# Attention logits on 64 rows of the array: products of hi of q and lo of k for two chunks of keys side by side

## The chip, the cores and the metric

The kernel runs on one core of a Trainium2 chip. The metric is the device time of one launch in microseconds (us). The kernel before takes 1200.92 us, the median of three runs (1200.59 to 1203.84). The engines have short names below: PE is TensorE's matmul and PEld its load of weights, DVE is VectorE, ACT is ScalarE, POOL is GpSimd, SP is SyncE, which only issues transfers here.

## What is computed

One layer of a decoder trunk on x of 1024 tokens by 1024 channels, float32: a norm, one projection, a gated spatial mixer on 4 groups of channels, a dilated causal attention on 12 heads of width 64, an output projection with a residual, and then a convolutional gated MLP. The attention is what the change touches. Cut to what matters:

```
logits = einsum('bnirhd,bnjrhd->bnrhij', qb, kc) * scale + bias      # scale = 1/8
logits = where(mask, logits, NEG_INF)
lse    = logsumexp(logits);  p = exp(logits - lse);  o = einsum(p, vc)
...                                                                  # three (window, dilation) pairs
o = sum(softmax(stack(lses)) * stack(outs))
```

The three dilated segments of a head share their logits, so the kernel works with one causal 1024 by 1024 matrix of logits per head, to which it adds one table that holds the position bias and the logarithm of how many segments contain each distance (-1e30 for none).

## The kernel before

**Numbers in two parts.** Float32 products run on TensorE in a rounded 32-bit type. To keep accuracy, each operand is split in two parts, hi (the rounded value) and lo (the rest), and a product is made of hi*hi, hi*lo and lo*hi, accumulated in one PSUM bank. For the logits the width of a head is only 64, so the array's 128 rows hold both parts of q at once: the tile Q has hi of q (times 1/8) in partitions 0 to 63 and lo of q in partitions 64 to 127. Kh has hi of k in both halves, Kl has lo of k in both halves. One matmul of Q with Kh gives hi*hi + lo*hi, one of Q with Kl gives hi*lo + lo*lo.

**One head.** `proj_qk` makes q and k of a head from the weights of both, 48 matmuls of 512 columns in two halves of 24 (tokens 0 to 511, then 512 to 1023). Behind each half `evac` takes PSUM apart: ScalarE writes hi of k (L483) and hi of q (L484), VectorE lo of k (L485) and lo of q (L486), and SP copies the k parts from partitions 64 to 127 into partitions 0 to 63 (L488, L489). The logits are made by `qk_row` for one block b of 128 queries against its 128*(b+1) keys: in one chunk up to block 3, in two chunks (`CH`) from block 4 on. A chunk has a PSUM bank of its own from a pool of three (`bS`), two matmuls (L511 with Kh, L512 with Kl), and then VectorE adds the bias and takes the running minimum of the negated row (L515). ScalarE takes the exponential (L520), VectorE the reciprocal of the sum (L522), POOL scales the row (L523). `tpv` transposes the rows (L543), splits them in hi and lo (L547 on ScalarE, L548 on VectorE) and multiplies with v (L565).

**Order.** TensorE and SP run in the order in which the code is written. The other engines' lists are put in order by a scheduler when the program is built, so code written for TensorE can move their rows too. A head is done in four steps g = 0 to 3. Each step issues one group of logits, two blocks (`qk_group`: group 0 is blocks 0 and 1, and so on to blocks 6 and 7), then the last product with v of the step before, then `tpv`. Groups 1, 2 and 3 of head h come in its steps 0, 1 and 2; group 0 of head h+1 comes in step 3 of head h. Between the pieces of `tpv`, `pump` issues matmuls of the next head's projection, in numbers from the table `FILL` (11, then 4+6+3, then 3+7+2+4, then 0+3+2+1+2), so the second half of head h's evacuation stands at the end of head h-1, just ahead of group 1 of head h, and the 11 projection matmuls come between group 1 and group 2.

**Buffers.** Q, Kh and Kl of all heads come from four buffers of 1024 columns (tag `qk`). The split weights of q and k (`wqh`, `wql`) have four buffers each of 512 columns, two per head; ScalarE makes the hi part and POOL the lo part.

Of the kernel before, what the change touches and what calls it, by code (L numbers as in the profile page):

```python
# [25 lines left out]
F = mybir.dt.float32  # L26
R = mybir.dt.float32r
# [5 lines left out]
T = 1024  # L33
# [29 lines left out]
def build(tc, x, g1, g2, g3, g4, w_in, ln_g, ln_b, sp_w, sp_b, rel, w_out, w_gate, w_up,  # L63
          conv_w, conv_b, w_down, onehot, lnm, out):
    nc = tc.nc
    pe, act, dve, pool, sp = nc.tensor, nc.scalar, nc.vector, nc.gpsimd, nc.sync
# [4 lines left out]
    def split(hi, lo, src, hi_eng, lo_eng):  # L71
        if hi_eng is act:
            act.activation(hi, src, AF.Copy)  # L73
        elif hi_eng is pool:
            pool.tensor_scalar(hi, src, 1.0, None, op0=OP.mult)
        else:
            dve.tensor_copy(hi, src)
        lo_eng.tensor_sub(lo, src, hi.bitcast(F))  # L78
# [6 lines left out]
    def open_pool(key, **kw):  # L85
        cms[key] = tc.tile_pool(name=key, **kw)
        return cms[key].__enter__()
# [4 lines left out]
    with tc.manual_schedule(engines={ET.PE, ET.SP}), \  # L92
# [8 lines left out]
        def bank(tag, n, nm):  # L101
            return ps.tile([128, 512], F, tag=tag, name=nm, bufs=n)

        def bS(nm):
            return bank("S", 3, nm)
# [7 lines left out]
        def bD(nm):  # L113
            return bank("D", 2, nm)
# [7 lines left out]
        def raw(nm):  # L122
            return rp.tile([128, 1024], F, tag="raw", name=nm)

        def stat(nm, n=1):
            return stp.tile([128, 4], F, tag="st", name=nm)[:, :n]
# [105 lines left out]
        def proj_a(key, n, i, nm, mid=None):  # L232
            p = bD(nm)
            s = slice(i * 128, (i + 1) * 128)
            for k in range(KT):
                if k == (6 if i == 0 else 4) and mid is not None:
                    mid()
                wh, wl = WT[key, k // 2]
                wh, wl = wh[:, k % 2, :], wl[:, k % 2, :]
                pe.matmul(p[:, :n], hTv(i, k, 0), wh, start=k == 0, stop=False)  # L240
                pe.matmul(p[:, :n], hTv(i, k, 0), wl, start=False, stop=False)  # L241
                pe.matmul(p[:, :n], hTv(i, k, 1), wh, start=False, stop=k == KT - 1)  # L242
            return p
# [77 lines left out]
        for i in range(NT):  # L321
# [23 lines left out]
            p = proj_a("uv", 512, i, "uv%d" % i, mid)  # L345
# [70 lines left out]
        for i in range(NT):  # L416
            p = proj_a("v0", 384, i, "v0_%d" % i)
# [18 lines left out]
        ap = open_pool("ag", bufs=2, reuse_waits="tile")  # L436
        WQ, QK, BIAS, ROW = {}, {}, {}, {}

        def load_qk(h):
            r = raw("wqk%d" % h)  # L440
            rv = r.rearrange("p (k c) -> p k c", k=KT)
            for j, nm in enumerate("qk"):
                c0 = C0[nm] + h * 64
                sp.dma_start(rv[:, :, j * 64:(j + 1) * 64],
                             w_in[:, c0:c0 + 64].rearrange("(k p) c -> p k c", p=128))
            WQ[h] = []
            for s in range(2):
                wh = ap.tile([128, 512], R, tag="wqh", name="wqh%d_%d" % (h, s), bufs=4)
                wl = ap.tile([128, 512], R, tag="wql", name="wql%d_%d" % (h, s), bufs=4)
                split(wh, wl, r[:, s * 512:(s + 1) * 512], ENG[WQK_HI[s]], pool)  # L450
                WQ[h].append((wh, wl))

# [7 lines left out]
        def proj_qk(h):  # L460
            st = {}

            def mm(hf, k, j):
                def f():
                    if k == 0 and j == 0:
                        st[hf] = bD("qk%d_%d" % (h, hf))
                    wh, wl = WQ[h][k // 4]
                    c = slice((k % 4) * 128, (k % 4 + 1) * 128)
                    w = wl[:, c] if j == 2 else wh[:, c]
                    m = hT[hf, k // 2, j == 1][:, k % 2, :]  # L470
                    pe.matmul(st[hf], w, m, start=k == 0 and j == 0, stop=k == KT - 1 and j == 2)  # L471
                    if k == KT - 1 and j == 2:
                        evac(hf)
                return f

            def evac(hf):
                if hf == 0:
                    QK[h] = tuple(ap2.tile([128, T], R, tag="qk", name="%s%d" % (n, h), bufs=4)
                                  for n in ("Q", "Kh", "Kl"))
                q, kh, kl = QK[h]  # L480
                p = st[hf]
                s = slice(hf * 512, (hf + 1) * 512)
                act.activation(kh[64:128, s], p[64:128], AF.Copy)  # L483
                act.activation(q[0:64, s], p[0:64], AF.Copy, scale=0.125)  # L484
                dve.tensor_sub(kl[64:128, s], p[64:128], kh.bitcast(F)[64:128, s])  # L485
                dve.scalar_tensor_tensor(q[64:128, s], p[0:64], 0.125, q.bitcast(F)[0:64, s],  # L486
                                         op0=OP.mult, op1=OP.subtract)
                sp.dma_start(kh.bitcast(F)[0:64, s], kh.bitcast(F)[64:128, s])  # L488
                sp.dma_start(kl.bitcast(F)[0:64, s], kl.bitcast(F)[64:128, s])  # L489

            return [mm(hf, k, j) for hf in range(2) for k in range(KT) for j in range(3)]

# [6 lines left out]

        CH = {4: (256, 384), 5: (384, 384), 6: (384, 512), 7: (512, 512)}  # L500

        def qk_row(h, b):
            q, kh, kl = QK[h]
            w = 128 * (b + 1)
            t = ap2.tile([128, T], F, tag="row", name="row%d_%d" % (h, b), bufs=4)
            c0 = 0
            nm = 3.0e38
            for n in CH.get(b, (w,)):
                p = bS("s%d_%d_%d" % (h, b, c0))
                qs = q[:, b * 128:(b + 1) * 128]  # L510
                pe.matmul(p[:, :n], qs, kh[:, c0:c0 + n], start=True, stop=False)  # L511
                pe.matmul(p[:, :n], qs, kl[:, c0:c0 + n], start=False, stop=True)  # L512
                nn = stat("nm%d_%d_%d" % (h, b, c0))
                o = 128 * (7 - b) + c0
                dve.tensor_tensor_reduce(t[:, c0:c0 + n], p[:, :n], BIAS[h][:, o:o + n], -1.0, nm,  # L515
                                         op0=OP.add, op1=OP.min, accum_out=nn)
                nm = nn
                c0 += n
            z = stat("z%d_%d" % (h, b))
            act.activation(t[:, :w], t[:, :w], AF.Exp, bias=nm, scale=-1.0, accum_out=z)  # L520
            rz = stat("rz%d_%d" % (h, b))
            dve.reciprocal(rz, z)  # L522
            pool.tensor_scalar(t[:, :w], t[:, :w], rz, 1.0, op0=OP.mult, op1=OP.mult)  # L523
            ROW[h, b] = t

        def qk_group(h, g):
            qk_row(h, 2 * g)
            qk_row(h, 2 * g + 1)

        def tpv(h, g, nfill):  # L530
            pair, odd = divmod(h, 2)
# [49 lines left out]

        bias_copies(0)
        load_qk(0)
        load_bias(0)
        for i in range(NT):
            p = proj_a("v1", 384, i, "v1_%d" % i)
            v_out(1, i, p)
            if i == 0:
                load_qk(1)
                bias_copies(1)  # L590
                bias_copies(2)
        close_pool("sa")
        ap2 = open_pool("ag2", bufs=4, side="right", reuse_waits="tile")
# [32 lines left out]
        fill.extend(proj_qk(0))  # L626
        pump(48)
        qk_group(0, 0)
        fill.extend(proj_qk(1))
        
        last_pv = lambda: None
        for h in range(HEADS):
            if h + 1 < HEADS:
                load_bias(h + 1)
            if h + 2 < HEADS:
                load_qk(h + 2)
# [5 lines left out]
            for g in range(4):  # L642
                if g < 3:
                    qk_group(h, g + 1)
                elif h + 1 < HEADS:
                    qk_group(h + 1, 0)
                if h == HEADS - 2:
                    if g == 0:
                        m0 = [mtile("ms0_%d" % s, R).rearrange("p (k c) -> p k c", k=KT) for s in range(2)]
                        mix_split(0, m0[0], m0[1], range(KT - 1))  # L650
                    for k in WO_AT[g]:
                        load_wo(k)
                if h == 0 and g == 0:
                    pump(FILL_FIRST)
                last_pv()
                last_pv = tpv(h, g, FILL_AT.get(h, FILL)[g])
                if g == 3 and h + 2 < HEADS:
                    fill.extend(proj_qk(h + 2))
                if g == 3 and h == HEADS - 2:
                    pump(len(fill))  # L660
                    for k in WO_AT[4]:
                        load_wo(k)
# [574 lines left out]
```

## Time and profile before

| | before |
|---|---|
| median of three runs | 1200.92 us (1200.59 to 1203.84) |
| the profiled execution | 1203.99 us, its span 1202.3 us, granted clock 0.992 |
| PE busy | 1160.8 us, 97% of the span |
| DVE busy | 841.0 us, 70% |
| ACT busy | 582.2 us, 48% |
| POOL busy | 380.2 us, 32% |
| logits matmuls | 144 of L511 and 144 of L512, from 159.8 to 451.5 us |
| one head, 180 to 350 us | 24.3 to 24.7 us |

How to read it: times in the timeline are start and duration in us from the start of the span. A busy PE is not PE at its peak: matmuls are pipelined, each shows a duration that overlaps the next one's start, so the distance between two starts is what a matmul costs. A remark in square brackets at the end of a row says how long the engine had been idle and what ended that.

### The profile page before, as it was taken

To read this page: it belongs to the slowest core of one execution; us is meant where nothing else is said; L and a number is where in the kernel's file an instruction comes from. 1 tells how busy PE (TensorE), PEld (TensorE's weight loads), DVE (VectorE), ACT (ScalarE), POOL (GpSimd) and SP (SyncE) were. 2 spreads that over 40 slices of the span, in tenths; PEclk is the share of its full clock that TensorE was granted. 3 is DMA by queue.
4 is the path that set the end of the run, shared out by engine and by line. 5 is a ranking of instruction groups with operands and counts; after the bars stand their busy time and mean duration, and the time that the engine had idled before them with its cause. 6 is when DMAs were issued, how large, how long until landed. Compare 5 with 4: busy or idle time off the path is not lost.

```text
span 1202.3 us, 16542 instructions
## 1 busy us (share of the span) xinstructions
PE 1160.8 (97%) x5687; PEld 975.2 (81%) x5687; DVE 841.0 (70%) x1559; ACT 582.2 (48%) x1172; POOL 380.2 (32%) x401
## 2 busy tenths in 40 slices
PE   6899999999999999998999999999999999999996
PEld 4789978888887878886778888888888888888884
DVE  5862257777777785468797777767777679679665
ACT  4532256666766665366443343433444245445521
POOL 3850023334323374234433223331233310000342
PEclk9999999999999999999999999999999999999999
DMA  5313032343233342341133314332243279334336
GB/s 194 108 59 101 13 83 73 91 118 82 73 77 79 104 141 71 109 154 53 35 116 113 98 69 131 103 126 76 91 132 96 86 281 371 107 97 120 112 116 227
DMA packets 107562, 134.83 MB, mean 112 GB/s; under 512 B 30794, under 2 KB 74326, under 8 KB 107478
## 3 DMA queue, kind: packets, MB, share of 16 engines
q1 hardware_dynamic: 105318, 131.93, 35.4%
q10 hardware_dynamic: 2160, 1.84, 0.4%
q8 instruction: 45, 0.74, 0.2%
q14 instruction: 39, 0.32, 0.1%
HBM read 98.82 MB, written 35.71 MB: 112 GB/s over the span
## 4 chain that ended last, share of the span: by engine, by line
PE 84%; DVE 6%; DMA 3%; POOL 2%; ACT 2%; issue 1%; SPq 1%; POOLq 0%; DVEq 0%; ACTq 0%
PE d L988 15%; PE qk L471 10%; PE y L622 7%; PE o L565 4%; PE pt L543 4%; PE s L511 2%; PE v L240 2%; PE s L512 2%; PE v L242 2%; PE v L241 2%; PE Bu L847 2%; PE Bu L849 2%; PE Bu L848 2%; PE Bg L849 2%; PE Bg L847 2%; PE Bg L848 2%
## 5 line engine op out<-in xcount | busy, mean ns | idle before, releaser
L988 PE MATMUL d<-t,s 128*128 128x512 f32 x924 | 210.4, 389 | 1.5 <-ACT t L73 1.2
L988 PEld LDWEIGHTS d<-t,s 128*128 128x128 f32 x924 | 173.3, 188 | 38.3 <-ACT t L73 1.6
L523 POOL TENSOR_SCALAR row<-row,rz 128x128 f32<-128x128 f32 (+3 forms) x96 | 73.1, 762 | 212.7 <-DVE rz L522 200.8
L520 ACT ACTIVATE row<-row,nm 128x128 f32<-128x128 f32 (+3 forms) x96 | 74.4, 775 | 48.6 <-DVE nm L515 48.3
L548 DVE TENSOR_TENSOR ptl<-pt,pth 128x512 fp32r<-128x512 f32 (+1 forms) x120 | 75.8, 634 | 19.3 <-ACT pth L547 17.9
L622 PE MATMUL y<-woh,ms 128*128 128x512 f32 x256 | 82.8, 396 | 0.4 <-DVE Q L486 0.4
L547 ACT ACTIVATE pth<-pt 128x512 fp32r<-128x512 f32 (+1 forms) x120 | 65.8, 550 | 33.3 <-PE pt L543 32.2
L471 PE MATMUL qk<-hTh,wqh 128*128 128x512 f32 x192 | 80.9, 421 | 0.0
L73 ACT ACTIVATE s<-sf 128x512 fp32r<-128x512 f32 x77 | 48.3, 627 | 66.1 <-PE d L988 26.2
L471 PE MATMUL qk<-hTl,wqh 128*128 128x512 f32 x192 | 78.7, 410 | 0.0
L471 PE MATMUL qk<-hTh,wql 128*128 128x512 f32 x192 | 76.6, 399 | 0.0
L78 DVE TENSOR_TENSOR s<-sf,s 128x512 fp32r<-128x512 f32 x77 | 56.4, 733 | 22.9 <-ACT s L73 22.8
L1003 POOL TENSOR_TENSOR x<-x,g4t 128x512 f32<-128x512 f32 x12 | 18.9, 1591 | 162.3 <-DMA g4t<-in_norm_ffn_post 133.5
L543 PE MATMUL pt<-ident,row 128*128 128x128 f32 x432 | 68.4, 274 | 1.7 <-POOL row L523 1.5
L73 ACT ACTIVATE wtg<-tg 128x512 fp32r<-128x512 f32 x44 | 27.6, 630 | 80.0 <-PE Cu L849 67.6
L797 POOL TENSOR_TENSOR tu<-wu 128x512 f32<-128x512 f32 x11 | 15.3, 1388 | 149.3 <-PE Ag L849 75.5
L900 DVE SCALAR_TENSOR_TENSOR c<-G,cols,c 128x1023 f32<-128x1023 f32 (+1 forms) x44 | 57.7, 1327 | 6.7 <-ACT c L898 6.7
L515 DVE CUSTOM_DVE_ANT_0 row<-s,bias 128x384 f32<-128x384 f32 (+2 forms) x96 | 49.9, 519 | 17.7 <-PE s L512 12.4
L73 ACT ACTIVATE wtu<-tu 128x512 fp32r<-128x512 f32 x44 | 27.6, 630 | 67.5 <-PE Cg L849 50.8
L543 PEld LDWEIGHTS pt<-ident,row 128*128 128x128 f32 x432 | 51.2, 140 | 10.6 <-POOL row L523 2.7
L622 PEld LDWEIGHTS y<-woh,ms 128*128 128x128 f32 x256 | 47.9, 188 | 10.8 <-issue 0.8
L565 PE MATMUL o<-ptl,V 128*128 128x256 f32 x240 | 49.5, 288 | 4.8 <-DVE ptl L548 4.6
(338 smaller groups left out, 3238.6 us busy)
## 6 DMA issues: line engine op xcount, KB each, us to landing
sf<-sD SPq DMA_DIRECT2D x77, 256.0 KB, 2.8
wu<-in_w_up SPq DMA_DIRECT2D x11, 1024.0 KB, 5.1
wd<-in_w_down SPq DMA_DIRECT2D x22, 512.0 KB, 7.2
wg<-in_w_gate SPq DMA_DIRECT2D x10, 1024.0 KB, 5.9
sD<-c SPq DMA_DIRECT2D x30, 256.0 KB, 6.6
gcop<-gd SPq DMA_DIRECT2D x12, 576.0 KB, 4.9
wqk<-in_w_in SPq DMA_DIRECT2D x24, 256.0 KB, 6.0
bias<-gcop SPq DMA_DIRECT2D x12, 512.0 KB, 3.8
```

The lines of the kernel that those rows point to most:

```text
L73: act.activation(hi, src, AF.Copy)
L78: lo_eng.tensor_sub(lo, src, hi.bitcast(F))
L471: pe.matmul(st[hf], w, m, start=k == 0 and j == 0, stop=k == KT - 1 and j == 2)
L520: act.activation(t[:, :w], t[:, :w], AF.Exp, bias=nm, scale=-1.0, accum_out=z)
L523: pool.tensor_scalar(t[:, :w], t[:, :w], rz, 1.0, op0=OP.mult, op1=OP.mult)
L543: pe.transpose(p[:, a * 128:(a + 1) * 128], r[:, jj * 128:(jj + 1) * 128], ident)
L547: act.activation(hi[:, :n], p[:, :n], AF.Copy)
L548: dve.tensor_sub(lo[:, :n], p[:, :n], hi.bitcast(F)[:, :n])
L565: pe.matmul(ov, v, t[:, s], start=j == 0 and x == 0, stop=x == 1 and j == 2 * g + 1, skip_group_check=True)
L622: pe.matmul(YP[i, hf], m, w, start=k == 0 and j == 0, stop=k == KT - 1 and j == 2)
L900: dve.scalar_tensor_tensor(c[:, d:T], g[:, 0:T - d], col(2 - d, f), c[:, d:T], op0=OP.mult, op1=OP.add)
L988: pe.matmul(b, l, r, start=first and n in FIRST and q == 0, stop=last and n in LAST and q == 2, skip_group_check=True)
```

## The change

The second matmul of a chunk now multiplies hi of q with lo of k alone; the product of lo of q and lo of k is left out. It needs only 64 of the array's rows. For two chunks the full matmuls with Kh come first, one behind the other, and then the two small ones: the first chunk's with rows 0 to 63, the second's with rows 64 to 127. For that there is a fourth tile per head, KQ: lo of k in partitions 0 to 63 and hi of q in partitions 64 to 127. The first chunk takes hi of q from Q and lo of k from KQ, the second takes hi of q from KQ and lo of k from Kl. The two chunks are the two blocks of a group for groups 0 and 1, and the two chunks of a block for groups 2 and 3.

SP now issues three copies per half of the evacuation instead of two: hi of k as before, lo of k into KQ, and hi of q into KQ. The buffers of tag `qk` go from four to five, those of `wqh` and `wql` from four to three each. All sizes of chunks, the fill table and the number of matmuls are as before.

```diff
-                wh = ap.tile([128, 512], R, tag="wqh", name="wqh%d_%d" % (h, s), bufs=4)
-                wl = ap.tile([128, 512], R, tag="wql", name="wql%d_%d" % (h, s), bufs=4)
+                wh = ap.tile([128, 512], R, tag="wqh", name="wqh%d_%d" % (h, s), bufs=3)
+                wl = ap.tile([128, 512], R, tag="wql", name="wql%d_%d" % (h, s), bufs=3)
...
-                    QK[h] = tuple(ap2.tile([128, T], R, tag="qk", name="%s%d" % (n, h), bufs=4)
-                                  for n in ("Q", "Kh", "Kl"))
-                q, kh, kl = QK[h]
+                    QK[h] = tuple(ap2.tile([128, T], R, tag="qk", name="%s%d" % (n, h), bufs=5)
+                                  for n in ("Q", "Kh", "Kl", "KQ"))
+
+                q, kh, kl, kq = QK[h]
...
                 sp.dma_start(kh.bitcast(F)[0:64, s], kh.bitcast(F)[64:128, s])
-                sp.dma_start(kl.bitcast(F)[0:64, s], kl.bitcast(F)[64:128, s])
+                sp.dma_start(kq.bitcast(F)[0:64, s], kl.bitcast(F)[64:128, s])
+                sp.dma_start(kq.bitcast(F)[64:128, s], q.bitcast(F)[0:64, s])
...
+        def qk_mm(h, jobs):
+            q, kh, kl, kq = QK[h]
+            ps_ = []
+            for b, c0, n in jobs:
+                p = bS("s%d_%d_%d" % (h, b, c0))
+                pe.matmul(p[:, :n], q[:, b * 128:(b + 1) * 128], kh[:, c0:c0 + n], start=True, stop=False)
+                ps_.append(p)
+            for (b, c0, n), p, x, y, r in zip(jobs, ps_, (q, kq), (kq, kl), (slice(0, 64), slice(64, 128))):
+                pe.matmul(p[:, :n], x[r, b * 128:(b + 1) * 128], y[r, c0:c0 + n], start=False, stop=True)
+            return ps_
...
-            for n in CH.get(b, (w,)):
-                p = bS("s%d_%d_%d" % (h, b, c0))
-                qs = q[:, b * 128:(b + 1) * 128]
-                pe.matmul(p[:, :n], qs, kh[:, c0:c0 + n], start=True, stop=False)
-                pe.matmul(p[:, :n], qs, kl[:, c0:c0 + n], start=False, stop=True)
+            for n, p in zip(CH.get(b, (w,)), ps_):
...
         def qk_group(h, g):
-            qk_row(h, 2 * g)
-            qk_row(h, 2 * g + 1)
+            bs = (2 * g, 2 * g + 1)
+            if g < 2:
+                ps_ = qk_mm(h, [(b, 0, 128 * (b + 1)) for b in bs])
+                for b, p in zip(bs, ps_):
+                    qk_row(h, b, [p])
+                return
+            for b in bs:
+                n0, n1 = CH[b]
+                qk_row(h, b, qk_mm(h, [(b, 0, n0), (b, n0, n1)]))
```

The second matmuls of a chunk stand at L514 in the changed kernel, the first ones at L511 as before. On the engines whose lists the scheduler orders, rows move too. On VectorE, around the first chunk of group 3 (row_6 is its first block, ptl_1_1 the lo part of the transposed rows of group 1), before:

```order
L515 ISA row_6_2652,nm_6_0_2656<-s_6_0_2653,bias_2175 128x384
L515 ISA nm_6_0_2656 128x1
L548 TENSOR_TENSOR ptl_1_1_2633<-pt_1_1_2628,pth_1_1_2632 128x384
L515 ISA row_6_2652,nm_6_384_2661<-s_6_384_2658,bias_2175,nm_6_0_2656 128x512
L515 ISA nm_6_384_2661 128x1
```

and now:

```order
L565 TENSOR_TENSOR ptl_1_1_2645<-pt_1_1_2640,pth_1_1_2644 128x384
L525 ISA row_6_2672,nm_6_0_2673<-s_6_0_2666,bias_2184 128x384
L525 ISA nm_6_0_2673 128x1
L525 ISA row_6_2672,nm_6_384_2675<-s_6_384_2668,bias_2184,nm_6_0_2673 128x512
L525 ISA nm_6_384_2675 128x1
```

The copy to ptl stands ahead of the block's first chunk instead of between its two chunks. On POOL the second of the two lo parts of the weights (wql_1) moves from ahead of block 6's scaling to behind it, ahead of block 7's:

```order
L78 TENSOR_TENSOR wql_0_2511<-wqk_2507,wqh_0_2510 128x512
L78 TENSOR_TENSOR wql_1_2515<-wqk_2507,wqh_1_2514 128x512
L523 TENSOR_SCALAR row_6_2652<-row_6_2652,rz_6_2665 128x896
L523 TENSOR_SCALAR row_7_2668<-row_7_2668,rz_7_2681 128x1024
```

and now:

```order
L78 TENSOR_TENSOR wql_0_2523<-wqk_2519,wqh_0_2522 128x512
L533 TENSOR_SCALAR row_6_2672<-row_6_2672,rz_6_2679 128x896
L78 TENSOR_TENSOR wql_1_2527<-wqk_2519,wqh_1_2526 128x512
L533 TENSOR_SCALAR row_7_2688<-row_7_2688,rz_7_2695 128x1024
```

Its counterpart on ScalarE, the hi part, moves the same way. The lists of TensorE and SP are shown in the prediction, at the places that it speaks of.

More of the change, by code (lines that the diff above doesn't have):

```diff
@@ L500, in build, with qk_row @@
         CH = {4: (256, 384), 5: (384, 384), 6: (384, 512), 7: (512, 512)}
-        def qk_row(h, b):
-            q, kh, kl = QK[h]
+        def qk_mm(h, jobs):
[8 more added lines that the diff above has]
+            return ps_
+        def qk_row(h, b, ps_):
             w = 128 * (b + 1)
```

## The prediction

> **What bounds the kernel now.** I read the page first, then the busy times of single heads, then one head's instructions in order of time. The first row is the page's; the two below it are from the view by stretches, each cut from one head's first logits matmul to the next head's.
>
> ```profile
> PE 1160.8 (97%) x5687; PEld 975.2 (81%) x5687; DVE 841.0 (70%) x1559; ACT 582.2 (48%) x1172; POOL 380.2 (32%) x401
> ...
> 204.87:229.47 24.60, 24.60 (x150) 21.25 (x149) 18.00 (x51) 17.09 (x37) 8.69 (x11) 1.00 0.37 89
> 229.47:253.80 24.33, 24.33 (x150) 21.19 (x149) 17.95 (x50) 16.86 (x36) 8.34 (x10) 1.00 0.36 90
> ```
>
> A head takes 24.3 to 24.6 us, TensorE is covered for all of it at full clock, and VectorE has work for 18.0. So time saved on TensorE is saved, and each wait that TensorE takes on is lost. The change touches four places of a head, its groups 0 to 3 of logits. Here are rows of groups 1 to 3 of one head from the timeline:
>
> ```profile
> 235.35 0.34 PE L511 MATMUL s<-Kh,Q 128*128 128x384 f32 x1
> ...
> 236.18 0.34 PE L565 MATMUL o<-pth,V 128*128 128x256 f32 x2
> ...
> 237.34 0.46 SPq L489 DMA_DIRECT2D Kl<-Kl  x1
> ...
> 237.85 0.58 SPq L456 DMA_DIRECT2D bias<-gcop  x1
> ...
> 239.46 0.28 PE L511 MATMUL s<-Kh,Q 128*128 128x256 f32 x1
> ...
> 239.58 0.28 PE L512 MATMUL s<-Kl,Q 128*128 128x256 f32 x1
> ...
> 239.70 0.34 PE L511 MATMUL s<-Kh,Q 128*128 128x384 f32 x1
> ...
> 239.88 0.33 PE L512 MATMUL s<-Kl,Q 128*128 128x384 f32 x1
> ...
> 240.01 0.42 DVE L515 CUSTOM_DVE_ANT_0 row<-s,bias 128x256 f32<-128x256 f32 x1
> ...
> 240.49 0.19 PEld L511 LDWEIGHTS s<-Kh,Q 128*128 128x128 f32 x1 [0.25 <-DVE nm L515]
> 240.49 0.45 PE L511 MATMUL s<-Kh,Q 128*128 128x384 f32 x1
> ...
> 240.78 0.34 PE L512 MATMUL s<-Kl,Q 128*128 128x384 f32 x1
> ...
> 240.95 0.34 PE L565 MATMUL o<-pth,V 128*128 128x256 f32 x2
> ...
> 245.64 0.33 PE L511 MATMUL s<-Kh,Q 128*128 128x384 f32 x1
> ...
> 246.13 0.47 ACT L547 ACTIVATE pth<-pt 128x384 fp32r<-128x384 f32 x1
> ...
> 246.30 0.56 DVE L515 CUSTOM_DVE_ANT_0 row<-s,bias 128x384 f32<-128x384 f32 x1 [0.92 <-PE s L512]
> 246.42 2.55 POOL L78 TENSOR_TENSOR wql<-wqk,wqh 128x512 fp32r<-128x512 f32 x2
> ...
> 246.78 0.55 DVE L548 TENSOR_TENSOR ptl<-pt,pth 128x384 fp32r<-128x384 f32 x1
> ...
> 246.92 0.50 PE L511 MATMUL s<-Kh,Q 128*128 128x512 f32 x1
> ...
> 247.26 0.39 PE L512 MATMUL s<-Kl,Q 128*128 128x512 f32 x1
> ...
> 247.49 0.34 PE L565 MATMUL o<-pth,V 128*128 128x256 f32 x2
> ```
>
> Matmuls overlap, so the price of one is the distance to the next start: 256 columns 0.12 us (239.46 to 239.58), 384 columns 0.175 (239.70 to 239.88), 512 columns 0.23 (247.26 to 247.49). The fourth chunk of a group waits: there are three PSUM banks, it gets the first chunk's, and VectorE must have read that one. The chain can be priced: the chunk's last matmul starts at 239.58 and runs 0.28, VectorE starts 0.15 later, takes 0.42, and TensorE goes 0.06 later, at 240.49. The matmul after such a wait takes 0.29 (240.49 to 240.78) where 0.175 is normal: 0.11 more, about one load of weights that nothing covers. Groups 1, 2 and 3 take 0.83, 1.49 and 1.85 us (235.35 to 236.18, 239.46 to 240.95, 245.64 to 247.49).
>
> **What it removes.** The second product of two chunks runs on two halves of the array at once, so the shorter of each pair is free: 0.175 in group 1 (384 beside 512), 0.12 + 0.175 in group 2, 0.175 + 0.23 in group 3, together 0.88 us per head. Group 0 (128 beside 256) I count at nothing: it still loads weights four times, and four times 0.11 is all that its matmuls need anyway.
>
> **What it adds, first: switching the array.** Each pair goes from 128 rows to 64 and back, six times a head. Matmuls with fewer rows stand in the trace in one place, the bias product with 32 rows; matmuls of another kind with all rows are the transposes.
>
> ```profile
> 88.13 0.34 PE L242 MATMUL v<-whv,hTl 128*128 128x384 f32 x1
> 88.40 0.81 PE L368 MATMUL bias<-bb 32*12 32x384 f32 x2
> 89.14 0.44 PE L240 MATMUL v<-whv,hTh 128*128 128x384 f32 x1
> 89.42 0.34 PE L241 MATMUL v<-wlv,hTh 128*128 128x384 f32 x1
> ...
> 242.34 0.60 PE L543 MATMUL pt<-ident,row 128*128 128x128 f32 x4
> 242.69 0.47 PE L471 MATMUL qk<-hTh,wqh 128*128 128x512 f32 x1
> 243.00 0.39 PE L471 MATMUL qk<-hTl,wqh 128*128 128x512 f32 x1
> ```
>
> The matmul ahead of the bias product is followed after 0.27 (0.095 over 0.175), the first one behind it after 0.28 (0.105 over): 0.20 there and back. The bias product also changes kind. Behind transposes the first matmul has 0.31 against 0.23, 0.08 for the kind alone. I take the difference, 0.12 for the rows (0.06 on the way in, 0.06 on the way out), with 0 and 0.20 as ends. The Trainium skill has a rule that speaks against this change: in TensorEngine Tiling (Array Packing), Key Properties, it says that changing the tiling mode, not just the tile, drains TensorE; it gives no time, the bias rows agree, and by the rule the price is above 0.
>
> **Second: a later first chunk.** The order of instructions on TensorE in group 3 of a head (s_6 and s_7 are its two blocks; Q, Kh, Kl and KQ are operands), before and now:
>
> ```order
> L511 MATMUL s_6_0_2653<-Kh_2311,Q_2310 128x384
> L512 MATMUL s_6_0_2653<-Kl_2312,Q_2310 128x384
> L511 MATMUL s_6_384_2658<-Kh_2311,Q_2310 128x512
> L512 MATMUL s_6_384_2658<-Kl_2312,Q_2310 128x512
> L511 MATMUL s_7_0_2669<-Kh_2311,Q_2310 128x512
> L512 MATMUL s_7_0_2669<-Kl_2312,Q_2310 128x512
> L511 MATMUL s_7_512_2674<-Kh_2311,Q_2310 128x512 [waits DVE_49]
> L512 MATMUL s_7_512_2674<-Kl_2312,Q_2310 128x512
> ```
>
> ```order
> L511 MATMUL s_6_0_2666<-Kh_2320,Q_2319 128x384
> L511 MATMUL s_6_384_2668<-Kh_2320,Q_2319 128x512
> L514 MATMUL s_6_0_2666<-KQ_2322,Q_2319 128x384
> L514 MATMUL s_6_384_2668<-Kl_2321,KQ_2322 128x512
> L511 MATMUL s_7_0_2682<-Kh_2320,Q_2319 128x512
> L511 MATMUL s_7_512_2684<-Kh_2320,Q_2319 128x512 [waits DVE_49]
> L514 MATMUL s_7_0_2682<-KQ_2322,Q_2319 128x512
> L514 MATMUL s_7_512_2684<-Kl_2321,KQ_2322 128x512
> ```
>
> The first chunk is now complete one full matmul later, and the wait stands two places earlier. Start the group at 0: the first chunk's second product starts at 0.175 + 0.23 + 0.06 = 0.47, VectorE could start at 0.47 + 0.33 + 0.15 = 0.95. On VectorE the ptl copy of 0.55, which ran behind that chunk at 246.78, is now queued ahead of it; one of the two weight copies on ScalarE ahead of its input moved back, so I put its end at 1.0. Then 0.56 for the chunk and 0.06: the fourth chunk starts at 1.62 (before: 1.28). Behind it 0.34 (246.92 to 247.26), 0.06, 0.23 and 0.06: the group ends at 2.3, not 1.85: **+0.47**, saving included. Without switches and ptl it is 2.08, +0.23.
>
> **Third: a transfer more.** SP's list for the second half of a head's evacuation, before and now:
>
> ```order
> L488 DMA Kh_2311<-Kh_2311 64x512 [waits DMAHW3_49,Activation_49]
> L489 DMA Kl_2312<-Kl_2312 64x512 [waits DMAHW4_49,DVE_49]
> L456 DMA bias_2505<-gcop 128x1024 [waits DMAHW5_49]
> ```
>
> ```order
> L489 DMA Kh_2320<-Kh_2320 64x512 [waits DMAHW7_49,Activation_49]
> L490 DMA KQ_2322<-Kl_2321 64x512 [waits DMAHW1_49,DMAHW0_49,DMAHW2_49,DVE_49,PE_49]
> L491 DMA KQ_2322<-Q_2319 64x512 [waits Activation_49]
> L489 DMA Kh_2320<-Kh_2320 64x512 [waits Activation_49]
> L490 DMA KQ_2322<-Kl_2321 64x512 [waits DMAHW3_49,DVE_49]
> L491 DMA KQ_2322<-Q_2319 64x512 [waits DMAHW4_49,Activation_49]
> L456 DMA bias_2517<-gcop 128x1024 [waits DMAHW5_49]
> ```
>
> The last rows are the second half; the copy of Q is new, stands behind the one from Kl, and group 2's second chunk needs it. The time to landing is in the view of the tile Kl:
>
> ```profile
> DMA to landing us min/median/max: 2.2/2.3/2.4
> ```
>
> Kl is made on VectorE behind the first chunk of group 1, which is late by 0.23 + 0.06: its issue goes from 237.34 to 237.63, the copy of Q 0.51 later (237.85 less 237.34), at 238.14, and lands at 240.44. TensorE wants it at 239.8. Behind the landing come 0.11 for the weights, 0.175 and 0.06; 0.175 twice, 0.06, 0.175 and 0.06: end at 241.43 instead of 240.95, and group 2 began 0.05 earlier: **+0.53**. The bank of group 2 is free before TensorE comes to it, so these waits don't add up. If the copy were in time, the bank alone would cost 0.18.
>
> **The rest.** Group 0: **+0.12**. Group 1: 0.12 less 0.175, **-0.05**. Fewer buffers for the weights move a 1.3 us copy on POOL (half of the row at 246.42) and a 0.6 us one on ScalarE in front of block 7; POOL is busy for 8.3 of 24.3 us, so I count nothing; without that cover it would be up to 0.6 per head. The load of bias starts 0.5 later, still 15 us before its use at 253.80, where the second stretch above ends. In return TensorE now waits for block 7 at the end of a head:
>
> ```profile
> 254.84 0.78 PE L543 MATMUL pt<-ident,row 128*128 128x128 f32 x4
> 255.38 0.48 PE L471 MATMUL qk<-hTl,wqh 128*128 128x512 f32 x1
> ```
>
> Four transposes take 0.54 there against 0.35 at 242.34; a later TensorE finds the block ready: **-0.2**.
>
> Sum per head: 0.47 + 0.53 + 0.12 - 0.05 - 0.2 = +0.87 us. Times eleven (the last two heads load W_out and I count them as one): +9.5 us. The profiled execution took 1203.99 us with a span of 1202.3; the median is 1200.92, so the sum gives 1213.5 by the one and **1210** by the other.
>
> **Rivals.** *The waits are there, switching is free and the copies come in time*: 0.18 + 0.23 - 0.175 - 0.2 per head, about 0, 1201; with the late copy in group 2 (0.24 more, worked out as above without switches) 1204. For it: nothing in the trace has 64 rows. Against: 32 rows cost 0.2.
> *The halves don't run side by side* (the change doesn't do what it says): group 1 gains no 0.175, the second rows of groups 2 and 3 lose 0.175 and 0.23, another 0.58 per head, 1216. For it: the weights of the second half are loaded while the first multiplies, and nothing shows that both run.
> *Faster*: the halves overlap, and the wait for the bank grows by less than what is saved: the full 0.88 on twelve heads, 10.6 us, 1190. It decides if VectorE starts on a first chunk early enough that group 3's fourth chunk starts before 1.28 - 0.175 = 1.1 instead of 1.62; against it stands the chain at 239.58 to 240.49. The Trainium skill would side with the overlap: TensorE: Matmul & The Clock Gate, Part 3, has matmuls on different row groups start about 4 ns apart; no row here shows it.
>
> **How the numbers follow.** Forecast 0.46 (1205 to 1214), free switching 0.21 (1200 to 1205), no overlap 0.17 (1213 to 1219), faster 0.13 (1188 to 1197), others 0.03. The range 1200 to 1218 leaves out the faster case and the worst of the third. A change of 0.3% (3.6 us) is about what can be told: slower than that are the forecast, the third and a third of the second, 0.71; the rest of the second is the same, 0.15; faster 0.14.
>
> **What would show it.** Starts of the two L514 matmuls a few ns apart: they overlap; 0.175 or more: they don't. The matmul ahead of a pair and the one behind it some 0.06 long: the switch. A load of weights at L511 waiting on VectorE for 0.5 us or more in group 3, and one at L514 for the copy of Q in group 2. A head of 25.3 us. Heads at 23.6 would make it wrong, as would a head no longer than now with none of these waits.

## The result

The changed kernel takes 1232.43 us (median of four runs, 1226.57 to 1233.76) against 1202.38 us for the kernel before (median of four, 1200.59 to 1204.42): a ratio of 1.024, with an interval of 1.021 to 1.026. The forecast was slower, 1210 us in a range of 1200 to 1218. The direction came true, the size did not: the loss is about 30 us where 9.5 was forecast.

The page of the changed kernel, and two heads of it from the view by stretches (length, then busy time of PE, PEld, DVE, ACT and POOL, the granted clock and DMA):

```profile
PE 1184.2 (96%) x5687; PEld 970.7 (79%) x5687; DVE 841.1 (68%) x1559; ACT 579.3 (47%) x1172; POOL 370.4 (30%) x401
...
234.10:260.70 26.60, 26.08 (x150) 20.53 (x149) 18.35 (x51) 16.84 (x37) 8.52 (x11) 1.00 0.37 92
260.70:290.86 30.16, 27.77 (x150) 21.66 (x149) 18.43 (x51) 16.54 (x37) 8.52 (x11) 0.94 0.34 81
```

A usual head has grown from 24.3 to 24.7 us to 26.6, and TensorE is no longer covered for all of it. Two heads of twelve are far longer (30.2 and 31.8 us); the second row is one of them. The kernel before has a long head too, the one from 351.74, with 29.0 us: there a ptl copy on VectorE stands behind three rows of 2.9 us in all at 367.31, which split the attention's output for the next projection, and TensorE waits 2.7 us for the copy. The changed kernel takes 27.1 us for that head. Of the 28.5 us between the two traces, the two long heads have 12.7 (against the same heads before), and this one gives back 1.9. The other engines do what they did.

Where a head lost it, read as starts of matmuls. First group 1, the cleanest one, since it waits for nothing (PE rows of the timeline; a row with x2 merges two matmuls):

```profile
240.30 0.57 PE L511 MATMUL s<-Kh,Q 128*128 128x384 f32 x2
240.81 0.44 PE L514 MATMUL s<-KQ,Q 64*128 64x384 f32 x1
240.81 0.49 PE L514 MATMUL s<-Kl,KQ 64*128 64x512 f32 x1
241.23 0.45 PE L582 MATMUL o<-pth,V 128*128 128x256 f32 x2
241.52 0.39 PE L582 MATMUL o<-ptl,V 128*128 128x256 f32 x2
```

The two 64-row matmuls start together (4 ns apart in the trace): they do run side by side. But the two full matmuls ahead of them take 0.51 us instead of 0.175 + 0.23, so 0.10 more; the pair takes 0.42 instead of 0.23, 0.19 more; and the two matmuls behind it take 0.29 where the same two took 0.17 before (236.18 to 236.35 there), 0.11 more. One stay in the 64-row mode costs 0.40 us. The group is 0.93 us long instead of 0.82, and 0.11 of its price lies behind it. The loads of weights at the two ends show part of it (PEld rows):

```profile
240.80 0.18 PEld L514 LDWEIGHTS s<-KQ,Q 64*128 64x128 f32 x1 [0.31 <-issue]
241.23 0.30 PEld L582 LDWEIGHTS o<-pth,V 128*128 128x128 f32 x2 [0.24 <-issue]
```

Both start only with their matmul, after 0.31 and 0.24 us of idle time in which they waited for nothing that the profile shows; before, the load for the matmul at 239.58 started at 239.47, under the matmul ahead of it. So the loads at the two ends of a stay are not covered.

Group 3, TensorE and then VectorE:

```profile
251.72 0.57 PE L511 MATMUL s<-Kh,Q 128*128 128x384 f32 x2
252.22 0.44 PE L514 MATMUL s<-KQ,Q 64*128 64x384 f32 x1
252.22 0.50 PE L514 MATMUL s<-Kl,KQ 64*128 64x512 f32 x1
252.65 0.50 PE L511 MATMUL s<-Kh,Q 128*128 128x512 f32 x1
253.43 0.49 PE L511 MATMUL s<-Kh,Q 128*128 128x512 f32 x1 [0.28 <-DVE nm L525]
253.85 0.50 PE L514 MATMUL s<-KQ,Q 64*128 64x512 f32 x1
...
254.28 0.45 PE L582 MATMUL o<-pth,V 128*128 128x256 f32 x2
```

```profile
252.26 0.56 DVE L565 TENSOR_TENSOR ptl<-pt,pth 128x384 fp32r<-128x384 f32 x1 [1.34 <-ACT pth L564]
252.81 0.56 DVE L525 CUSTOM_DVE_ANT_0 row<-s,bias 128x384 f32<-128x384 f32 x1
```

The fourth chunk starts 1.71 us into the group (251.72 to 253.43; forecast 1.62, before 1.28), behind VectorE's read of the first one. That read ran from 252.81, right behind the ptl copy queued ahead of it. The group takes 2.56 us instead of 1.85. Group 2:

```profile
244.62 0.46 PE L511 MATMUL s<-Kh,Q 128*128 128x256 f32 x2
245.01 0.38 PE L514 MATMUL s<-KQ,Q 64*128 64x256 f32 x1
245.63 0.44 PE L514 MATMUL s<-Kl,KQ 64*128 64x384 f32 x1 [0.24 <-DMA KQ<-Q]
245.99 0.62 PE L511 MATMUL s<-Kh,Q 128*128 128x384 f32 x2
246.54 0.44 PE L514 MATMUL s<-KQ,Q 64*128 64x384 f32 x1
...
246.91 0.45 PE L582 MATMUL o<-pth,V 128*128 128x256 f32 x2
```

The pair falls apart: its second half starts 0.62 us behind the first because the copy of hi of q has not landed. The group takes 2.29 us here, 2.36 in the median over the heads, instead of 1.49.

Over the heads from 175 to 400 us the medians of the groups, and of the stretches between them, are (worked out from the starts in the traces; the stretch behind a group begins at the first matmul that is not a logits matmul):

| us per head | group 0 | 1 | 2 | 3 | behind 0 | behind 1 | behind 2 | behind 3 |
|---|---|---|---|---|---|---|---|---|
| before | 0.46 | 0.82 | 1.49 | 1.84 | 5.69 | 3.29 | 4.69 | 6.32 |
| changed | 0.64 | 0.93 | 2.36 | 2.57 | 5.56 | 3.40 | 4.81 | 6.42 |
| new order, all with 128 rows | 0.46 | 0.82 | 2.16 | 2.57 | 5.53 | 3.29 | 4.71 | 6.33 |
| 64 rows in the old order | 1.03 | 1.50 | 2.75 | 3.21 | 5.45 | 3.40 | 4.82 | 6.42 |
| fewer weight buffers alone | 0.46 | 0.81 | 1.49 | 1.99 | 6.35 | 3.29 | 4.69 | 6.33 |

The last three rows are experiments, told next. Some medians stand for two lengths that alternate from head to head: before, the stretch behind group 0 (5.43 and 5.7, mean 5.58); in the new order, groups 2 and 3 (2.03 and 2.30, 2.43 and 2.70); with fewer buffers, group 3 (1.85 and 2.13).

### The profile page after: what moved, and what is told of

The parts are those of the page before. It is cut to its first block, busy times and chain, and to the rows that moved or that the text cites. A ratio compares the mean times of both kernels' runs of the same rounds, so it can differ in the third digit from the quotient of the medians.

```text
span 1230.8 us, 16563 instructions
## 1 busy us (share of the span) xinstructions
PE 1184.2 (96%) x5687; PEld 970.7 (79%) x5687; DVE 841.1 (68%) x1559; ACT 579.3 (47%) x1172; POOL 370.4 (30%) x401
## 3 DMA queue, kind: packets, MB, share of 16 engines
q10 hardware_dynamic: 2160, 1.84, 0.4%
## 4 chain that ended last, share of the span: by engine, by line
PE 68%; DVE 4%; DMA 3%; POOL 1%; ACT 1%; issue 1%; SPq 0%; POOLq 0%; DVEq 0%; ACTq 0%
PE d L1005 15%; PE y L639 7%; PE qk L471 5%; PE o L582 3%; PE pt L560 2%; PE Bu L866 2%; PE Bg L866 2%; PE Bu L864 2%; PE Bu L865 2%; PE Bg L864 2%; PE Bg L865 2%; PE Ag L866 2%; PE Cu L866 2%; PE Au L866 2%; PE Cg L866 2%; PE Ag L865 2%
## 5 line engine op out<-in xcount | busy, mean ns | idle before, releaser
L814 POOL TENSOR_TENSOR tu<-wu 128x512 f32<-128x512 f32 x11 | 19.8, 1802 | 152.5 <-PE Ag L866 78.3
L78 POOL TENSOR_TENSOR wql<-wqk,wqh 128x512 fp32r<-128x512 f32 x24 | 30.9, 1288 | 83.4 <-ACT wqh L73 66.8
```

## The experiments

Two theories to begin with. **S**: the switches of the array cost most of the loss. **W**: the waits do, for the bank and for the copy of hi of q. Each ratio is to the kernel before, run again on the same chip; its median there was 1201.69 to 1203.81 us, so a microsecond or two between two experiments says little.

### The copy of hi of q first

```diff
-                sp.dma_start(kq.bitcast(F)[0:64, s], kl.bitcast(F)[64:128, s])
                 sp.dma_start(kq.bitcast(F)[64:128, s], q.bitcast(F)[0:64, s])
+                sp.dma_start(kq.bitcast(F)[0:64, s], kl.bitcast(F)[64:128, s])
```

> The changed kernel, with the copy of hi of q into KQ issued ahead of the copy of lo of k instead of behind it; nothing else. In the changed kernel group 2 of a head stands still for about 0.5 us because that copy lands late. Theory S (the switches of the array between 128 and 64 rows cost most of the loss, about 0.39 us for each of six pairs a head: 0.09 on the way in, 0.19 behind the pair, 0.11 on the first matmul after it): the wait goes, the wait for the bank of the same group takes over in part, about 0.27 us a head is won, 1229 us. Theory W (the waits for the copy and the bank are most of the loss of 2.2 us a head): over 0.8 us a head is won, under 1222 us.

1226.31 us, ratio 1.020 (1.018 to 1.022), about 6 us less than the changed kernel: between the two theories. But the gain is not where it was expected. Group 2 with the copy in time:

```profile
217.72 0.46 PE L511 MATMUL s<-Kh,Q 128*128 128x256 f32 x2
218.11 0.38 PE L514 MATMUL s<-KQ,Q 64*128 64x256 f32 x1
218.11 0.44 PE L514 MATMUL s<-Kl,KQ 64*128 64x384 f32 x1
218.48 0.44 PE L511 MATMUL s<-Kh,Q 128*128 128x384 f32 x1
219.37 0.45 PE L511 MATMUL s<-Kh,Q 128*128 128x384 f32 x1 [0.45 <-DVE nm L525]
```

The halves are together again, and the 0.6 us come back at once as a wait for the bank: 0.89 us from 218.48 to 219.37. Group 2 is 2.27 us in the median, 0.09 shorter. A usual head stays at 26.5 to 26.7. What went are the two long heads (27.1 and 26.8 us here). In the changed kernel's long head:

```profile
271.80 0.38 PE L514 MATMUL s<-KQ,Q 64*128 64x256 f32 x1
...
274.30 0.44 PE L514 MATMUL s<-Kl,KQ 64*128 64x384 f32 x1 [2.12 <-DMA KQ<-Q]
```

```profile
275.20:278.60 3.40, 3.40 (x12) 2.55 (x12) 1.83 (x8) 1.30 (x3) 0.80 (x1) 0.52 1.00 236
```

The pair's second half starts 2.5 us behind the first, which is 1.9 more than in a usual head, and the next 3.4 us ran at a granted clock of 0.52 (first number behind POOL's). A second trace of the changed kernel was taken for this:

> The changed kernel once more, for its trace. In its profiled execution the copy of hi of q landed 2.4 us too late in two of twelve heads, which cost 3.5 and 4.7 us in these heads. If that belongs to the kernel, the same heads are long again (30 us and more) and the time is 1230 to 1234 us; if it is chance, other heads or none, and about 1226 us where none is.

1227.33 us, and the same head is long again, 31.56 us, with the pair's second half 2.5 us late; the second long head was not. In both traces a transfer of 16 KB on the queue that the profile calls instruction (program code) starts while the copy is due, at 271.36 and at 271.08 us; in the first one another starts at 408.38, in the other long head. In the view of transfers of the changed kernel, cut to 271.35 to 271.45 us, it is the second queue (packets, MB, share of 16 engines):

```profile
q1 hardware_dynamic: 16, 0.03, 146.0%
q8 instruction: 1, 0.02, 86.9%
```

The single packets in the traces show more than a coincidence. The copy is 64 packets of 2 KB. In the first case 60 have started by 271.93 us; the last four start one behind the other from 272.74, and the code transfer ends at 272.75 (1.39 us long). In the other two cases the last four start from 409.63 and 272.72, and the code transfers end at 409.63 and 272.73. In the second trace, in the head that was the other long one in the first, the copy is issued at 408.31 and its last packet starts 1.45 us later; a code transfer starts at 410.19, behind it, and nothing is late. So the end of the copy stood behind the code transfer. Whether one falls on a copy that TensorE is about to need is timing: with hi of q first, none did in its trace. No run moves a code transfer alone.

### The order alone

The kernel before with the new order; the lines are set against those of the changed kernel, and KQ and its copy are gone as well:

```diff
...
                 pe.matmul(p[:, :n], q[:, b * 128:(b + 1) * 128], kh[:, c0:c0 + n], start=True, stop=False)
...
-            for (b, c0, n), p, x, y, r in zip(jobs, ps_, (q, kq), (kq, kl), (slice(0, 64), slice(64, 128))):
-                pe.matmul(p[:, :n], x[r, b * 128:(b + 1) * 128], y[r, c0:c0 + n], start=False, stop=True)
+            for (b, c0, n), p in zip(jobs, ps_):
+                pe.matmul(p[:, :n], q[:, b * 128:(b + 1) * 128], kl[:, c0:c0 + n], start=False, stop=True)
```

> The kernel before, with the new order alone: both matmuls with Kh of a pair of chunks first, then both matmuls with Kl, all with 128 rows; no KQ, no copy of q, no 64-row matmul, buffers as before. It has the later first chunk and the longer wait for the bank, and no switch. Theory S: group 2 ends at 1.84 instead of 1.49 us, group 3 at 2.37 instead of 1.85, 0.2 comes back at the end of the head: about +0.6 us a head, 1209 us. Theory W: most of the 2.2 us a head, 1222 us or more.

1219.38 us, ratio 1.014 (1.012 to 1.015). Between the two: the order costs 16 us, more than half of the loss, without one 64-row matmul. Group 2 on TensorE and VectorE:

```profile
216.48 0.45 PE L509 MATMUL s<-Kh,Q 128*128 128x256 f32 x2
216.77 0.55 PE L512 MATMUL s<-Kl,Q 128*128 128x256 f32 x2
217.15 0.34 PE L509 MATMUL s<-Kh,Q 128*128 128x384 f32 x1
218.14 0.45 PE L509 MATMUL s<-Kh,Q 128*128 128x384 f32 x1 [0.65 <-DVE nm L523]
```

```profile
215.30 0.43 DVE L593 TENSOR_TENSOR mix<-o,ot 64x256 f32<-64x256 f32 x1
...
217.54 0.16 DVE L530 RECIPROCAL rz<-z 128x1 f32<-128x1 f32 x1 [0.41 <-ACT row L528]
217.65 0.42 DVE L523 CUSTOM_DVE_ANT_0 row<-s,bias 128x256 f32<-128x256 f32 x1
```

The first chunk is complete at 216.77 + 0.28, so by the chain of before VectorE could read it at 217.2. It reads it at 217.65, because its list has the reciprocal of block 3 ahead, and that one waits for ScalarE. Block 3's own chain is late because group 1's first chunk is late by 0.23 and a sum of 0.43 (mix) now stands ahead of it. So the chunk that opens the bank is late twice: by TensorE's order, and by what that did to VectorE's list. This is one of the longer groups 2 (2.30 us); in the shorter ones (2.03) the same reciprocal stands there and ends 0.27 sooner. Group 3 is held up by the ptl copy ahead of its first chunk, as in the changed kernel: in every other head the fourth chunk starts 1.63 us into the group, in the others 1.89, because ScalarE delivers the copy's input later.

### The switches alone

```diff
-                pe.matmul(p[:, :n], qs, kl[:, c0:c0 + n], start=False, stop=True)
+                pe.matmul(p[:, :n], q[0:64, b * 128:(b + 1) * 128], kl[0:64, c0:c0 + n], start=False, stop=True)
```

> The kernel before in its own order, with the second product of every chunk made from hi of q and lo of k on rows 0 to 63 alone (the product of lo of q and lo of k is left out); nothing runs side by side, nothing is saved, the copies are those of before. It switches the array twelve times a head there and back instead of six times. Theory S: 12 times 0.39 is 4.7 us a head, less what the waits of before hide, some 0.3: 1250 us or a little more. Theory W: no wait is longer than before by more than a switch hides, at most 0.5 us a head, 1207 us.

1248.86 us, ratio 1.038 (1.036 to 1.039); a head takes 28.6 us, 4.1 more for twelve stays, 0.34 each net of what the waits hide. Theory S has the price of a switch right, within 2 us of its sum. One stay:

```profile
216.83 0.50 PE L511 MATMUL s<-Kh,Q 128*128 128x512 f32 x1
217.26 0.50 PE L512 MATMUL s<-Kl,Q 64*128 64x512 f32 x1
217.69 0.45 PE L565 MATMUL o<-pth,V 128*128 128x256 f32 x2
```

A single 64-row matmul of 512 columns takes 0.43 us, as long as a pair: 0.20 more than 0.23, with nothing beside it.

### Both halves on the same rows

On top of the run with the copy of hi of q first:

```diff
...
-            for (b, c0, n), p, x, y, r in zip(jobs, ps_, (q, kq), (kq, kl), (slice(0, 64), slice(64, 128))):
+            for (b, c0, n), p, x, y, r in zip(jobs, ps_, (q, q), (kq, kq), (slice(0, 64), slice(0, 64))):
```

> The changed kernel with the copy of hi of q issued first, with both 64-row matmuls of a pair on rows 0 to 63, so that they cannot run side by side. If the overlap is worth what the starts 3 to 4 ns apart say: each pair gets longer by the shorter product, 0.06 to 0.23 us, and by a load of weights of 0.11; group 2's first and group 3's first hide in the wait for the bank, so about 0.8 us a head, 1235 us. If the side by side is worth nothing: 1226 us.

1230.82 us against 1226.31 with the halves side by side: the overlap is worth some 5 us, half of what was expected. Much of the rest hides in the wait for the bank: group 2 grows by 0.08 us where its two shorter products take 0.30, group 3 by 0.22 where they take 0.41. This run also takes the price of a stay apart. In group 3 (its pairs start at 228.16 and 229.81 us in the trace) the first of the pair takes 0.28 with 384 columns, 0.11 more than normal, the last one 0.32 with 512, 0.09 more. So each way costs 0.09 to 0.10 on the last matmul of the old mode and 0.11 on the first of the new one, the amount that an uncovered load of weights costs after a wait: 0.20 in, 0.20 out.

### Fewer buffers for the weights alone

```diff
-                wh = ap.tile([128, 512], R, tag="wqh", name="wqh%d_%d" % (h, s), bufs=4)
-                wl = ap.tile([128, 512], R, tag="wql", name="wql%d_%d" % (h, s), bufs=4)
+                wh = ap.tile([128, 512], R, tag="wqh", name="wqh%d_%d" % (h, s), bufs=3)
+                wl = ap.tile([128, 512], R, tag="wql", name="wql%d_%d" % (h, s), bufs=3)
```

> The kernel before with three instead of four buffers each for the hi and lo parts of the weights of q and k, which moves a 1.3 us copy on POOL and a 0.6 us copy on ScalarE in front of block 7. Theory S and theory W as the prediction had it: POOL is a third busy and the copies are hidden, 1201 us. A third theory, that this late copy holds up block 7: up to 0.6 us a head, 1208 us.

1209.44 us, ratio 1.006 (1.004 to 1.008), 6 to 7 us: as much as the third theory said, but not at its place. In the view of waits from 180 to 360 us (total, times, longest) TensorE waits for a ptl copy:

```profile
PE o L565 <- DVE ptl L548: 3.3, 6, 0.8
```

Before, that view shows no wait of TensorE's matmuls at all in this stretch. The copy is that of blocks 4 and 5, not of block 7. VectorE at the end of a head, with fewer buffers and then before:

```profile
256.38 0.16 DVE L522 RECIPROCAL rz<-z 128x1 f32<-128x1 f32 x1 [0.91 <-ACT row L520]
256.98 0.29 DVE L515 CUSTOM_DVE_ANT_0 row<-s,bias 128x128 f32<-128x128 f32 x1 [0.44 <-PE s L512]
...
257.49 0.56 DVE L548 TENSOR_TENSOR ptl<-pt,pth 128x384 fp32r<-128x384 f32 x1 [0.20 <-DVE nm L515]
```

```profile
253.57 0.16 DVE L522 RECIPROCAL rz<-z 128x1 f32<-128x1 f32 x1 [0.77 <-ACT row L520]
253.94 0.56 DVE L548 TENSOR_TENSOR ptl<-pt,pth 128x384 fp32r<-128x384 f32 x1 [0.21 <-ACT pth L547]
254.62 0.29 DVE L515 CUSTOM_DVE_ANT_0 row<-s,bias 128x128 f32<-128x128 f32 x1
```

The copy now stands behind the next head's first read, which needs a chunk that TensorE makes just before it wants the copy. The weight copy on POOL itself ends in time (256.59, the reciprocal that block 7 needs at 256.54). So moving the weight copies changed VectorE's list, and the list made the wait. In the changed kernel the ptl copy stands ahead of that read, as before (260.95 and 261.48), and the stretch behind group 0 is 5.56 us, not 6.35: this cost doesn't show there. The changed kernel uses the room of these buffers for KQ, and no run has it with both.

### Work for TensorE during the wait

Three projection matmuls of the next head are put between the two blocks of groups 2 and 3, and taken from the fill that follows.

```diff
...
             for b in bs:
+                if b % 2:
+                    pump(3)
                 n0, n1 = CH[b]
```

> The changed kernel with the copy of hi of q issued first, and with three matmuls of the next head's projection (0.7 us) put between the two blocks of groups 2 and 3, taken from the fill that follows, so that TensorE has work while VectorE reads the first chunk. If the loss is made of waits for the bank (0.7 us a head in group 2 and 0.55 in group 3) plus switches: the waits go, the switches stay, 1.2 us a head less than without the fill (1226), 1213 us. If the switches alone made it: no change, 1226 us.

> The new order alone, all with 128 rows, with the same three matmuls between the blocks of groups 2 and 3. If waits for the bank are all that the order costs (16 us), they go: 1202 us, and the difference to the run with 64-row pairs and the same fill is the price of six switches a head less the 0.88 us saved, about 1.4 us a head, 16 us before waits. If the order costs otherwise (VectorE's list): still above 1210 us.

1221.79 us (64-row pairs, copy first) and 1216.84 us (128 rows). A usual head fell to 25.6 and 24.8 us, but the logits of the last head took some 10 us longer than in the kernel before in both traces (30.0 and 29.8 us against 19.5), so the same was run with the fill in heads 0 to 9 only:

> The changed kernel with the copy of hi of q first and three projection matmuls between the blocks of groups 2 and 3, but only in heads 0 to 9. In the run with the fill in all heads a steady head fell to 25.6 us from 26.6, but head 11, whose fill is the output projection, took 10 us more, because the moved matmuls came before their operands. Without that: about 1211 us. If the 10 us are not due to the fill in the last heads: 1221 us again.

> The new order with 128 rows throughout and the same fill in heads 0 to 9. A steady head with that fill was 24.8 us against 24.5 before and 25.9 without fill. Without the loss in head 11: about 1207 us; the difference to the run with 64-row pairs and the same fill, 0.75 us a head and 8 us in all, is what six switches a head cost beyond the 0.88 us saved, with the part that hides in waits taken off. If the loss in head 11 is not due to the fill: 1217 us again.

1216.78 us, ratio 1.011 (1.009 to 1.013), and 1212.01 us, ratio 1.006 (1.004 to 1.008). Both are some 5 us better, not 10: without a fill the new order itself takes 3 to 4 us more in the last head than the kernel before (23.5 and 22.6 us in the two runs without fill). The usual heads, first without fill (128 rows), then with it, 128 rows and 64:

```profile
232.23:258.08 25.85, 24.79 (x150) 21.24 (x149) 18.05 (x51) 16.75 (x36) 8.33 (x11) 1.00 0.34 84
```

```profile
230.11:254.93 24.82, 24.66 (x151) 21.45 (x150) 18.01 (x51) 16.97 (x37) 8.51 (x10) 1.00 0.35 88
```

```profile
230.93:256.53 25.60, 25.60 (x151) 20.38 (x149) 18.14 (x51) 16.79 (x37) 8.64 (x11) 1.00 0.39 96
```

With 128 rows the fill takes away 1.0 of the 1.4 us a head that the order costs: these were waits. With 64 rows it takes away 1.0 as well, and what stays is 0.8 us a head above the 128-row order with the same fill, with TensorE covered throughout: the switches, less the saving and less what they hide. By the price of a stay 1.5 us would be due (six times 0.40, less 0.88); the other 0.7 stands against waits that the 128-row run keeps, and no run takes that apart.

### Pairs in groups 0 and 1 only

```diff
...
             for b in bs:
-                n0, n1 = CH[b]
-                qk_row(h, b, qk_mm(h, [(b, 0, n0), (b, n0, n1)]))
+                ps_, c0 = [], 0
+                for n in CH[b]:
+                    p = bS("s%d_%d_%d" % (h, b, c0))
+                    qs = q[:, b * 128:(b + 1) * 128]
+                    pe.matmul(p[:, :n], qs, kh[:, c0:c0 + n], start=True, stop=False)
+                    pe.matmul(p[:, :n], qs, kl[:, c0:c0 + n], start=False, stop=True)
...
```

> Half of the change alone: 64-row pairs in groups 0 and 1, while groups 2 and 3 keep the order and the 128-row products of before; buffers and copies of the changed kernel, hi of q first. Two switches a head at 0.39 less 0.175 saved in group 1, so 0.6 us on groups 0 and 1; up to 0.25 of it comes back at the end of the head where TensorE waits for block 7 anyway, unless the later copy of the weights eats that. Switches as measured: 0.4 to 0.6 us a head, 1206 to 1209 us. If a switch cost 0.12 as predicted: +0.07 a head, 1202 us.

The second matmuls of groups 2 and 3 take lo of k from Kl again, and hi of q is still copied last here, behind lo of k; TensorE doesn't wait for that copy. 1215.41 us, ratio 1.010 (1.008 to 1.013): a miss, 6 us above. Groups 0 and 1 behave as expected (0.64 and 0.93 us), but groups 2 and 3, unchanged in their code, grow to 1.84 and 2.10, and the view of waits from 180 to 380 us has them behind VectorE:

```profile
PEld s L549 <- DVE nm L525: 9.2, 16, 0.9
```

Group 1's late first chunk pushes VectorE's list into group 2, as in the run of the order alone: the same reciprocal stands there (216.12 us, after 0.41 us of waiting for ScalarE). Group 3 alternates between 1.88 and 2.11 us, much as with fewer buffers alone (1.85 and 2.13), where group 2 stays at 1.49. So by these two runs group 3's part goes with the buffers, and group 2's doesn't.

### The fill on the kernel before

```diff
...
             qk_row(h, 2 * g)
+            if g >= 2:
+                pump(1)
             qk_row(h, 2 * g + 1)
```

> The kernel before with one matmul of the next head's projection (0.23 us) between the two blocks of groups 2 and 3, taken from the fill behind them. The kernel before waits about 0.1 us for the bank in each of these groups and pays 0.11 for the load of weights behind it. If the wait can be filled: 0.4 us a head, 1197 us. If it only moves to another place: 1202 us.

1203.89 us, ratio 1.001 (1.000 to 1.003): the same. A head is 24.3 to 24.5 us; the view of waits no longer has the fourth chunk's wait, but a usual head is hardly shorter. No run came out faster than the kernel before.

## Why the prediction was right and wrong

**Right**: that TensorE bounds each head; that the halves run side by side, so the rival without overlap is out; the mechanism of a later first chunk and a wait for its bank; the late copy of q in group 2, and that it doesn't add to the bank's wait (taking it away gave 0.09 us a head). **Half right**: the 0.2 us back at the end of the head. It was read at 254.84, in a head whose stretch behind group 0 takes 5.78 us; every other head of before has 5.43. Now it is 5.56, with 0.11 of a switch in it: about 0.2 back in the one kind of head, nothing in the other.

**Wrong in size, by 1.2 us a head** (0.87 forecast, 2.1 measured). By the terms of the sum, forecast and measured with the stretch behind each group: group 3 +0.47 and +0.83, group 2 +0.53 and +0.99, group 1 -0.05 and +0.22, group 0 with the end of the head -0.08 and +0.05. Two steps failed:

*The price of a switch*, 0.12 there and back, ends 0 and 0.20. It is 0.40. The step that failed is the reading of the bias product: it counted the matmul ahead and the one behind, 0.20, and left out the two merged bias matmuls between them, the first in the new mode and the last. The row showed them: from 88.40 to 89.14 they take 0.74 us, where two of 384 columns take 0.35. (How much of that 0.39 is the rows and how much the other kind, that row can't say.) Then 0.08 was taken off for the change of kind. The runs show 0.10 on the way in and 0.09 on the way out, and 0.11 more each time for weights that nothing covers. Six stays are 2.4 us a head against 0.88 saved. The Trainium skill (TensorEngine Tiling (Array Packing), Key Properties) says that a change of tiling mode drains TensorE. Every pair measured here agrees with that, at 0.40 us a stay. For group 1, for which the sum had -0.05, this price gives +0.22 (0.11 within it and 0.11 behind), for group 0 0.29 instead of 0.12.

*The wait for the bank.* The order alone was good for 0.35 in group 2 and 0.52 in group 3 by the prediction's chain, and cost 0.67 and 0.73. The chain of before (0.15, 0.42, 0.06) was right; the step that failed is that VectorE is free when the chunk is complete. In group 2 a reciprocal that waits for ScalarE stands ahead, late because of group 1. In group 3 the prediction had the ptl copy ahead of the chunk and its end at 1.0; that holds in every other head of the order alone, and in the changed kernel it ends at 1.09.

The waits and the switches hide in one another in groups 2 and 3: the changed kernel's group 3 is as long as that of the order alone (2.57), and its group 2 is 0.2 longer. That is why the order alone costs 16 us, pairs with the copy in time 7 more, and the late copy another 6. The last 6 us are in the main the two long heads, of which the prediction had nothing: it counted on a landing of 2.3 us every time.

**Counted at nothing, rightly or not**: the weight copy in front of block 7 would have cost 0.6 per head without cover, the prediction said; alone it costs 6 to 7 us in all (0.66 behind group 0 and 0.15 in group 3). That cost comes from a ptl copy that moved on VectorE, not from block 7. The changed kernel's list has the copy at its old place, and its 5.56 us behind group 0 don't show the cost: counted at nothing rightly, by the luck of a list.

**Rivals.** Free switching fell with 0.40. No overlap fell with the common starts, and with the 5 us that halves on the same rows cost. Faster needed a fourth chunk of group 3 before 1.1 us; it starts at 1.71.

## What to carry to other kernels

A stay in the 64-row mode costs 0.40 us here, with one matmul in it or a pair, so six short stays a head, 2.4 us, don't pay for the 0.88 that they save. By this price a stay pays only if what runs in it saves more than 0.40 us; no run here has such a stay. Before products are regrouped, follow the first result to its reader and the bank to its next writer, and ask what stands ahead of that reader in its list; the order alone cost 16 us here, and the pairs, with what they saved and what the waits hid, 7. Read the lists of the other engines again after each change: two of these costs came from rows that moved on VectorE. A price read off at the edges of a merged group of instructions is a lower end, not an upper one.

## What was not expected of the hardware

A 64-row matmul alone takes as long as two side by side (0.43 us for 512 columns), since the price belongs to the stay. A copy within the core landed 2.3 us after its issue in most heads (2.6 at most in the view of line L491, which leaves out the late ones). Where a 16 KB transfer of program code started before the copy's last four packets, these four waited until it ended, and TensorE went on over 4 us after the issue (270.05 to 274.30). A wait of 2.0 to 2.1 us on TensorE was followed by 3.4 us at half the granted clock (0.50 to 0.52) in all three cases, and the 2.7 us wait in the long head of the kernel before as well (0.50 from 370.8 to 374.2), so that one late landing cost 3.5 us or more.
